# Triangular inverse in a two-block transformer kernel: row-by-row part on blocks of 8 instead of 16, and one more doubling level

## The chip, the cores and the metric

The kernel runs on one core of one Trainium2 chip. The metric is device time in microseconds of one execution. Before the change the three timed runs took 1562.48, 1565.49 and 1566.18 us; their median, 1565.49 us, is the time to compare with. One more execution was profiled; all rows below are from it.

## The reference, cut to what matters

The reference runs two layers of one model and one layer of another over 256 tokens of width 1024, in float32: feed-forward blocks, a gated delta rule mixer (8 heads), a sliding-window attention, and a last mixer that joins windowed attention with a linear recurrence in two directions (8 heads). The gated delta rule solves a unit lower triangular system in each chunk:

```
L = jnp.where(strict, jnp.einsum("bhnid,bhnjd->bhnij", kb, k) * decay, 0.0)
rhs = jnp.concatenate([v * beta[..., None], kb * jnp.exp(g)[..., None]], axis=-1)
sol = lax.linalg.triangular_solve(L, rhs, left_side=True, lower=True,
                                  transpose_a=False, conjugate_a=False, unit_diagonal=True)
```

and the recurrence of the last mixer is a scan over time steps:

```
sa = jnp.einsum('dbhij,dbhj->dbhi', state, a_t)
state = (state * w_t[..., None, :] + sa[..., :, None] * b_t[..., None, :]
         + v_t[..., :, None] * k_t[..., None, :])
y = jnp.einsum('dbhij,dbhj->dbhi', state, r_t)
```

The kernel does both in chunks, and in both it needs the inverse of a unit triangular matrix: 128x128 in the first mixer, 64x64 in the last.

## The kernel before, in words

Weights arrive as 512 KB blocks on one DMA queue (line 173). ScalarE rounds each block to a high part (line 177), VectorE forms the rest (line 178), and TensorE multiplies with both parts, three products for one (lines 181 to 184). These projections are nearly all of TensorE's work.

A mixer runs as a set of generators. `chain` (first mixer, one for each group of four heads) and `rw_chain` (last mixer, one for each pair of heads) hold the work in which each step waits for the one before; `stream` holds the projections. `weave` (lines 314 to 337) takes steps from both. A step yields two numbers: the TensorE time it takes, and the time until its result can be used. With these `weave` keeps a clock of its own and puts filler steps from the stream between a chain's step and its next one, until the clock has passed the second number times `slack`. In the last mixer TensorE's instructions keep exactly the order in which `weave` emits them (line 1510, slack 1.3, line 1511). In the first mixer (slack 1.1, line 792) a planner orders all engines by priority, and everywhere it orders VectorE and ScalarE. Each engine works its queue in order.

`tri_inverse` (lines 422 to 488) inverts eight triangular matrices at once, `nu = 8`, all four 32-row strips of the partitions side by side. It is called by `chain` twice in all and by `rw_chain` four times. Before the call ScalarE gathers the diagonal 32x32 blocks into `Lc` (lines 708 and 1196). Then:

- Lines 429 to 431: VectorE masks out the diagonal 16x16 blocks of `Lc` and adds the two halves, which gives `Ld`, 16 columns for each partition.
- Lines 433 to 440: the row-by-row part. For each row k a shuffle spreads row k of the block to its partitions (`irow`, line 438), a multiplication by the rows already found goes into `unit` (tile `iun`, line 439), and a reduction adds up (`iYc`, line 440). `unit` holds 1 + 2 + ... + 16 = 136 columns for each matrix; `inverse_scratch` fills it once for each mixer (line 419). All three operations grow with k.
- Lines 441 to 444: `iYc` is spread back into the diagonal blocks of `Y`, `Xt` is its transpose, and the step yields (0, 14.0).
- Lines 446 to 462: the doubling level from 16 to 32, on TensorE: 32 products `Lc`*`Y` into a bank, a masked copy `T` on VectorE (line 451), 64 products with `Xt` and `T`, and the two updates of `Y` and `Xt` on VectorE (lines 460 and 461).
- Lines 464 to 488: the level from 32 to 64, with ScalarE doing the copies.

A 32x32 float32 product shows in the profile as two matmul records and two weight loads. All matmuls of `mm` carry line 197 in the profile, whoever calls it.

The last mixer's head pairs overlap: the chain of pair t+1 prepares its operands (lines 1133 to 1139) while pair t inverts and scans.

Of the kernel before, what the change touches and what calls it, by code (L numbers as in the profile page):

```python
# [12 lines left out]
ALU = mybir.AluOpType  # L13
PSUM = bass.MemoryType.PSUM

P = 128
# [41 lines left out]
def _consts():  # L58
    i = np.arange(P)
    t, s = i[:, None], i[None, :]  # L60
    f = lambda m: m.astype(np.float32)


    half = np.concatenate([t // 16 % 2 == 0, t // 16 % 2 == 1], 1)
    unit = np.zeros((P, 136))
    for k in range(16):
        unit[:, k * (k + 1) // 2 + k] = i % 16 == k
    lev4 = (t % 32 < 16) & (np.arange(32)[None, :] >= 16)
    inv = [("half", f(half)), ("nhalf", -f(half)), ("lev4", f(lev4)), ("unit", unit)]
    groups = {  # L70
        "base": [("ident", f(t == s)), ("ones", np.ones((P, P), np.float32))],
        "delta": [("tri", f(t <= s)), ("maskA", np.where(s < t, NEG, 0.0)), ("maskL", np.where(s >= t, -NEG, 0.0))],
        "inv": inv,

        "swa": [("band", np.concatenate([np.where(s > t, 0.0, NEG), np.where(s <= t, 0.0, NEG)], 1))],

        "gqa": [(f"near{m}", np.where(np.abs(t + m * P - np.arange(256)[None, :]) <= P, 0.0, NEG)) for m in range(2)],
    }


    blk = t // 64 == s // 64
    groups["prep"] = [("triF", f(blk & (t <= s))), ("triB", f(blk & (t >= s))), ("sel", f(blk)[:, 0:65:64])]
    rw = []
    for d in range(2):
        m = np.zeros((P, 2, P), np.float32)
        for step in range(2):
            odd = step if d == 0 else 1 - step
            direct = np.arange(P) // 64 == odd
            at = np.where(direct | (d == 1), np.arange(P) % 64, 63 - np.arange(P) % 64)
            if d == 1:  # L90
                at = 63 - at
            m[:, step] = np.where(direct[None, :], at[:, None] <= at[None, :], at[:, None] < at[None, :])
        rw.append((f"m{d}", m.reshape(P, 2 * P)))
    groups["scan"] = rw
    half = 8
    inv = np.power(np.float32(500000.0), -np.arange(half, dtype=np.float32) * np.float32(2.0) / np.float32(16))
    ang = np.arange(256, dtype=np.float32)[:, None] * inv[None, :].astype(np.float32)
    cos, sin = np.cos(ang.astype(np.float32)), np.sin(ang.astype(np.float32))
    groups["gqa"] += [("cos", cos.reshape(2, P, half).transpose(1, 0, 2).reshape(P, 16)),
                      ("sin", sin.reshape(2, P, half).transpose(1, 0, 2).reshape(P, 16))]  # L100
    arrays, cols = {}, {}
    for g, parts in groups.items():
        at = 0
        for name, m in parts:
            cols[name] = (g, at, m.shape[1])
            at += m.shape[1]
        arrays["c_" + g] = np.ascontiguousarray(np.concatenate([m for _, m in parts], axis=1).astype(np.float32))
    return arrays, cols


CONSTS, CONST_COLS = _consts()


# [5 lines left out]
def _program(ctx, tc, a, out, stages):  # L119
    nc = tc.nc  # L120
# [10 lines left out]
    def bank(pool=None):  # L131
        pool = pool or psB
        return pool.tile([P, 512], F32, tag="A" if pool is psA else "B", name="bank")
# [17 lines left out]
    def C(name):  # L151
        g, o, n = CONST_COLS[name]
        return cst[g][:, o:o + n]
# [42 lines left out]
    def mm(o, lhsT, rhs, start=True, stop=True, **kw):  # L196
        nc.tensor.matmul(o, lhsT, rhs, start=start, stop=stop, **kw)  # L197
# [217 lines left out]
    q32 = [slice(32 * r, 32 * r + 32) for r in range(4)]  # L415

    def inverse_scratch(tl, nu):
        un = tl([nu, 136], "iun")
        nc.vector.tensor_copy(un, C("unit").unsqueeze(1).to_broadcast([P, nu, 136]))
        return un  # L420

    def tri_inverse(tl, Lc, off, nu, sign, unit, X, ydst=None):
        W = nu * 32
        uv = lambda y: y.rearrange("p (u s) -> p u s", u=nu)
        uf = lambda y: y.rearrange("p u s -> p (u s)")
        halves = lambda y: y.rearrange("p u (a s) -> p u a s", a=2)
        grid = lambda m: C(m).unsqueeze(1).unsqueeze(3).to_broadcast([P, nu, 2, 16])
        op = ALU.subtract if sign > 0 else ALU.add
        Lm, Ld = tl([nu, 32], "iLm"), tl([nu, 16], "iLd")
        nc.vector.tensor_tensor(halves(Lm), halves(Lc), grid("nhalf" if sign > 0 else "half"), ALU.mult)  # L430
        nc.vector.tensor_tensor(Ld, Lm[:, :, 0:16], Lm[:, :, 16:32], ALU.add)

        Yc = tl([nu, 16], "iYc")
        for k in range(16):
            o = k * (k + 1) // 2
            if k:
                row = tl([nu, 16], "irow", 2)[:, :, 0:k]
                nc.vector.stream_shuffle(row, Ld[:, :, 0:k], [i // 16 * 16 + k for i in range(32)])  # L438
                nc.vector.tensor_tensor(unit[:, :, o:o + k], row, Yc[:, :, 0:k], ALU.mult)
            nc.vector.tensor_reduce(Yc[:, :, k], unit[:, :, o:o + k + 1], mybir.AxisListType.X, ALU.add)  # L440
        Y, Xt = tl([nu, 32], "iY"), tl([nu, 32], "iX")
        nc.vector.tensor_tensor(halves(Y), Yc.unsqueeze(2).to_broadcast([P, nu, 2, 16]), grid("half"), ALU.mult)
        nc.vector.transpose(uf(Xt), uf(Y))
        yield 0, 14.0

        ps = bank()
        for u in range(nu):
            for r in q32:
                mm(ps[r, u * 32:u * 32 + 32], Lc[r, u], Y[r, u])
        T = tl([nu, 32], "iT")  # L450
        nc.vector.tensor_tensor(T, uv(ps[:, :W]), C("lev4").unsqueeze(1).to_broadcast([P, nu, 32]), ALU.mult)
        yield 0.15 * nu, 1.6
        ps = bank()
        for u in range(nu):
            for r in q32:
                mm(ps[r, u * 32:u * 32 + 32], Xt[r, u], T[r, u])
        for u in range(nu):
            for r in q32:
                mm(ps[r, W + u * 32:W + u * 32 + 32], T[r, u], Xt[r, u])
        nc.vector.tensor_tensor(Y, Y, uv(ps[:, :W]), op)  # L460
        nc.vector.tensor_tensor(Xt, Xt, uv(ps[:, W:2 * W]), op)
        yield 0.3 * nu, 1.6

        low, high = q32[0::2], q32[1::2]
        T = tl([nu, 32], "iT")
        ps = bank()
        for u in range(nu):
            for l, h in zip(low, high):
                mm(ps[l, u * 32:u * 32 + 32], off(u, h, l), Y[h, u])
        for l in low:  # L470
            nc.scalar.copy(T[l], uv(ps[l, :W]))
        for i, r in enumerate(q32):
            c = slice(i % 2 * 32, i % 2 * 32 + 32)
            nc.scalar.copy(X[r, :, c], Xt[r])
            if ydst:
                nc.scalar.copy(ydst(r)[:, :, c], Y[r])
        yield 0.08 * nu, 1.6
        ps = bank()
        for u in range(nu):
            for l, h in zip(low, high):  # L480
                mm(ps[h, u * 32:u * 32 + 32], T[l, u], Xt[l, u])
                if ydst:
                    mm(ps[l, u * 32:u * 32 + 32], Xt[l, u], T[l, u])
        for l, h in zip(low, high):
            nc.scalar.activation(X[h, :, 0:32], uv(ps[h, :W]), AF.Copy, scale=-float(sign))
            if ydst:
                nc.scalar.activation(ydst(l)[:, :, 32:64], uv(ps[l, :W]), AF.Copy, scale=-float(sign))
        yield 0.1 * nu, 1.6


    def deltanet():
# [4 lines left out]
        with tc.tile_pool(name="delta", bufs=1) as dp:  # L496
# [78 lines left out]

            conv = V("conv").rearrange("p (t j) -> p t j", j=4)
            unit = inverse_scratch(tl, 8)
            X64 = [tl([8, 64], f"X64{i}") for i in range(2)]
            Yf = [tl([8, P], f"Yf{i}") for i in range(2)]
# [123 lines left out]
            def chain(s):  # L703
# [3 lines left out]
                for r in q32:  # L707
                    nc.scalar.copy(Lc[r], L4[r, :, r])
                X, Y = X64[gr], Yf[gr]
                lo, hi = slice(0, 64), slice(64, P)  # L710
                yield from tri_inverse(tl, Lc, lambda u, h, l: L4[h, u, l], 8, 1, unit, X,
                                       lambda r: Y[r, :, (lo if r.start < 64 else hi)])
                ps = bank()
# [260 lines left out]
    def mixer2_body(tl, hT, rstd, sums, finish_norm):  # L974
# [71 lines left out]
        def rw_chain(t):  # L1046
# [146 lines left out]
            for r in q32:  # L1193
                for par in range(2):
                    Md = M[int(r.start // 64 == par)]
                    nc.scalar.copy(L4[r, :, par::2], Md[r, :, par::2, r])
            state["rw"][t] = 1
            yield from tri_inverse(tl, Lc, lambda u, h, l: M[int(h.start // 64 == u % 2)][h, u // 4, u % 4, l], 8, -1, unit,
                                   X64[t % 2])
            X = X64[t % 2]  # L1200
# [531 lines left out]
```

## Time and profile before

| what | before |
|---|---|
| median of 3 runs | 1565.49 us |
| the profiled execution's own time | 1568.78 us |
| its span (first to last instruction) | 1567.0 us |
| TensorE busy | 1510.5 us (96%) |
| VectorE busy | 1101.2 us (70%) |
| ScalarE busy | 918.8 us (59%) |
| mean granted TensorE clock | 0.984 |

A row of the timeline gives the start in us from the span's start, the time it took, engine, line, operation, what it writes and reads, shapes and the number of instructions merged; in brackets, for how long the engine had been idle before it and what ended that. PE is TensorE's matmul, PEld its weight load, DVE is VectorE, ACT is ScalarE, SPq the queue that issues the DMAs. Matmuls are pipelined, so a matmul's own time is longer than its distance to the next one; the distance is what it costs. "issue" stands for time in which an engine waited for nothing that the profile shows.

### The profile page before, as it was taken

What the parts mean: (1) busy time and instruction counts of PE and PEld (TensorE: products, weight loads), DVE (VectorE), ACT (ScalarE), POOL (GpSimd) and SP (SyncE); (2) the same over time, 40 slices, a digit from 0 to 9 for tenths busy, and PEclk for the clock granted to TensorE, in tenths of its full rate; (3) what the DMA queues carried; (4) which work ended last, traced back from release to release, by engine and by line L of the source; (5) the groups of instructions that cost most, each with busy time, mean ns of one, the idle gap of its engine ahead of it and who ended that gap; (6) DMA issues with size and microseconds to landing.
All of it is one profiled execution on the core that took longest, in us unless ns stands there. A gap on an engine that the chain in (4) does not pass through costs nothing.

```text
span 1567.0 us, 28074 instructions
## 1 busy us (share of the span) xinstructions
PE 1510.5 (96%) x10592; PEld 1298.8 (83%) x10592; DVE 1101.2 (70%) x2691; ACT 918.8 (59%) x2000; POOL 36.9 (2%) x51
## 2 busy tenths in 40 slices
PE   8999998999999999999999999999988988999998
PEld 6888887898888888888887888879977877778887
DVE  6766779686766667666666767667987865766665
ACT  6655576666655556555545655556767554655554
POOL 0000011011000000000100000000000000000000
PEclk9999998899999999999999999999999999999999
DMA  7766614243766647666432766646331222665551
GB/s 232 218 193 196 191 41 132 82 135 122 215 202 196 196 120 230 200 200 191 141 95 86 221 194 199 193 145 183 105 100 31 69 60 94 195 215 189 188 188 54
DMA packets 71192, 244.18 MB, mean 156 GB/s; under 512 B 8464, under 2 KB 12304, under 8 KB 71056
## 3 DMA queue, kind: packets, MB, share of 16 engines
q1 hardware_dynamic: 71056, 242.39, 51.0%
q8 instruction: 83, 1.36, 0.4%
q14 instruction: 53, 0.43, 0.1%
HBM read 241.31 MB, written 1.05 MB: 155 GB/s over the span
## 4 chain that ended last, share of the span: by engine, by line
PE 82%; DVE 9%; DMA 4%; ACT 3%; issue 1%; POOL 1%; SPq 0%; ACTq 0%; DVEq 0%; POOLq 0%
PE bank L189 22%; PE bank L197 12%; PE bank L182 12%; PE bank L184 12%; PE bank L183 11%; PE bank L190 11%; DVE wl L178 3%; DMA raw<-in_w_ff_dram 1%; ACT wh L177 1%; PE bank L248 1%; DMA raw<-in_ffn_w_dram 1%; DVE cacc L596 1%; DMA raw<-in_w_rwkv_dram 0%; DVE irow L438 0%; PE bank L851 0%
## 5 line engine op out<-in xcount | busy, mean ns | idle before, releaser
L178 DVE TENSOR_TENSOR wl<-raw,wh 128x512 fp32r<-128x512 f32 (+1 forms) x714 | 574.7, 828 | 219.2 <-ACT wh L177 213.3
L177 ACT CAST wh<-raw 128x512 fp32r<-128x512 f32 (+1 forms) x714 | 497.0, 731 | 286.5 <-DMA raw<-in_ffn_w_dram 173.6
L189 PE MATMUL bank<-hT,wh 128*128 128x512 f32 x1664 | 587.7, 396 | 3.7 <-DVE hT L255 3.2
L190 PE MATMUL bank<-hT,wl 128*128 128x256 f32 x1664 | 463.3, 279 | 0.1
L189 PEld LDWEIGHTS bank<-hT,wh 128*128 128x128 f32 x1664 | 312.8, 188 | 77.7 <-DVE hT L255 5.7
L190 PEld LDWEIGHTS bank<-hT,wl 128*128 128x128 f32 x1664 | 313.6, 188 | 4.9 <-DVE wl L178 0.6
L182 PE MATMUL bank<-wh,aT 128*128 128x512 f32 x584 | 233.4, 400 | 5.5 <-ACT aT L216 5.2
L184 PE MATMUL bank<-wh,aT 128*128 128x512 f32 x584 | 229.3, 396 | 1.2 <-DVE aT L217 1.1
L183 PE MATMUL bank<-wl,aT 128*128 128x512 f32 x584 | 229.1, 392 | 0.0
L182 PEld LDWEIGHTS bank<-wh,aT 128*128 128x128 f32 x584 | 110.1, 189 | 32.0 <-ACT aT L216 8.3
L184 PEld LDWEIGHTS bank<-wh,aT 128*128 128x128 f32 x584 | 109.8, 188 | 29.2 <-DVE aT L217 3.7
L183 PEld LDWEIGHTS bank<-wl,aT 128*128 128x128 f32 x584 | 110.3, 189 | 19.9
L182 PE MATMUL bank<-hT,wh 128*128 128x256 f32 x384 | 115.9, 302 | 0.0
L184 PE MATMUL bank<-hT,wl 128*128 128x256 f32 x384 | 111.0, 291 | 1.7 <-DVE wl L178 1.7
L183 PE MATMUL bank<-hT,wh 128*128 128x256 f32 x384 | 111.2, 290 | 0.0
L402 ACT ACTIVATE gs<-gs 128x256 f32<-128x256 f32 x88 | 36.7, 417 | 86.5 <-DVE gs L401 86.5
L194 DVE TENSOR_TENSOR av<-av,bank 128x256 f32<-128x256 f32 x120 | 50.0, 418 | 43.9 <-ACT av L193 43.2
L184 PEld LDWEIGHTS bank<-hT,wl 128*128 128x128 f32 x384 | 74.6, 195 | 3.8 <-DVE wl L178 2.4
L182 PEld LDWEIGHTS bank<-hT,wh 128*128 128x128 f32 x384 | 74.9, 195 | 2.8 <-issue 1.5
L183 PEld LDWEIGHTS bank<-hT,wh 128*128 128x128 f32 x384 | 75.0, 195 | 2.4 <-issue 2.0
L216 ACT CAST aT<-av 128x256 fp32r<-128x256 f32 x120 | 48.6, 406 | 20.8 <-DVE av L1555 12.0
L197 PE MATMUL bank<-wh,hT 128*128 128x256 f32 x256 | 57.6, 306 | 2.1 <-DVE hT L255 2.1
(415 smaller groups left out, 1940.0 us busy)
## 6 DMA issues: line engine op xcount, KB each, us to landing
raw<-in_ffn_w_dram SPq DMA_DIRECT2D x264, 512.0 KB, 4.2
raw<-in_w_ff_dram SPq DMA_DIRECT2D x64, 512.0 KB, 4.3
raw<-in_a_w_qkv_dram SPq DMA_DIRECT2D x24, 512.0 KB, 3.8
raw<-in_w_gate_dram SPq DMA_DIRECT2D x16, 512.0 KB, 3.5
raw<-in_w_rwkv_dram SPq DMA_DIRECT2D x14, 512.0 KB, 3.5
raw<-in_b_w_qk_dram SPq DMA_DIRECT2D x10, 512.0 KB, 4.2
raw<-in_a_w_z_dram SPq DMA_DIRECT2D x8, 512.0 KB, 3.6
raw<-in_a_w_out_dram SPq DMA_DIRECT2D x8, 512.0 KB, 3.5
```

Of the source, the lines that this page charges most:

```text
L177: nc.scalar.copy(hi[:, c], raw[:, c])
L178: nc.vector.tensor_tensor(lo[:, c], raw[:, c], hi.bitcast(F32)[:, c], ALU.subtract)
L182: nc.tensor.matmul(o, l[0], r[0], start=start, stop=False, **kw)
L183: nc.tensor.matmul(o, l[0], r[1], start=False, stop=False, **kw)
L184: nc.tensor.matmul(o, l[1], r[0], start=False, stop=stop, **kw)
L189: nc.tensor.matmul(o, l[0], both, start=start, stop=False, skip_group_check=True)
L190: nc.tensor.matmul(o[:, 0:256], l[1], both[:, 0:256], start=False, stop=stop, skip_group_check=True)
L194: nc.vector.tensor_tensor(t, t, o[:, 0:256], ALU.add)
L197: nc.tensor.matmul(o, lhsT, rhs, start=start, stop=stop, **kw)
L216: nc.scalar.copy(hi, src)
L248: nc.tensor.transpose(ps[:, q * 256 + h * P:q * 256 + (h + 1) * P], x[h][n][:, c * P:(c + 1) * P], ident)
L402: nc.scalar.activation(gs, gs, AF.Silu)
```

## The change: blocks of 8 row by row, and the doubling level run twice

The row-by-row part stops at row 7, with 36 columns of `unit` instead of 136. `Ld` is made by one reduction over four masked quarters instead of an addition of two halves. The doubling level on TensorE becomes a loop over two masks: `lev3` joins 8x8 blocks to 16x16, `lev4` joins 16x16 to 32x32 as before. Both use the same instructions. The first yield is (0, 7.5) instead of (0, 14.0). The constants have 108 columns instead of 172.

```
-        Lm, Ld = tl([nu, 32], "iLm"), tl([nu, 16], "iLd")
-        nc.vector.tensor_tensor(halves(Lm), halves(Lc), grid("nhalf" if sign > 0 else "half"), ALU.mult)
-        nc.vector.tensor_tensor(Ld, Lm[:, :, 0:16], Lm[:, :, 16:32], ALU.add)
-
-        Yc = tl([nu, 16], "iYc")
-        for k in range(16):
+        Lm, Ld = tl([nu, 32], "iLm"), tl([nu, 8], "iLd")
+        nc.vector.tensor_tensor(quarters(Lm), quarters(Lc), grid("nquart" if sign > 0 else "quart"), ALU.mult)
+        nc.vector.tensor_reduce(Ld, Lm.rearrange("p u (a s) -> p u s a", a=4), mybir.AxisListType.X, ALU.add)
+
+        Yc = tl([nu, 8], "iYc")
+        for k in range(8):
             o = k * (k + 1) // 2
             if k:
-                row = tl([nu, 16], "irow", 2)[:, :, 0:k]
-                nc.vector.stream_shuffle(row, Ld[:, :, 0:k], [i // 16 * 16 + k for i in range(32)])
+                row = tl([nu, 8], "irow", 2)[:, :, 0:k]
+                nc.vector.stream_shuffle(row, Ld[:, :, 0:k], [i // 8 * 8 + k for i in range(32)])
                 nc.vector.tensor_tensor(unit[:, :, o:o + k], row, Yc[:, :, 0:k], ALU.mult)
             nc.vector.tensor_reduce(Yc[:, :, k], unit[:, :, o:o + k + 1], mybir.AxisListType.X, ALU.add)
...
         nc.vector.transpose(uf(Xt), uf(Y))
-        yield 0, 14.0
-
-        ps = bank()
...
+        yield 0, 7.5
+
+        for lev in ("lev3", "lev4"):
+            ps = bank()
+            for u in range(nu):
+                for r in q32:
+                    mm(ps[r, u * 32:u * 32 + 32], Lc[r, u], Y[r, u])
+            T = tl([nu, 32], "iT")
+            nc.vector.tensor_tensor(T, uv(ps[:, :W]), C(lev).unsqueeze(1).to_broadcast([P, nu, 32]), ALU.mult)
+            yield 0.15 * nu, 1.6
+            ps = bank()
+            for u in range(nu):
+                for r in q32:
+                    mm(ps[r, u * 32:u * 32 + 32], Xt[r, u], T[r, u])
+            for u in range(nu):
+                for r in q32:
+                    mm(ps[r, W + u * 32:W + u * 32 + 32], T[r, u], Xt[r, u])
+            nc.vector.tensor_tensor(Y, Y, uv(ps[:, :W]), op)
+            nc.vector.tensor_tensor(Xt, Xt, uv(ps[:, W:2 * W]), op)
+            yield 0.3 * nu, 1.6
```

## Rows read from the trace of the kernel before

**Rows 1.** The page: busy time of each engine; shares of the chain of waits

```profile
PE 1510.5 (96%) x10592; PEld 1298.8 (83%) x10592; DVE 1101.2 (70%) x2691; ACT 918.8 (59%) x2000; POOL 36.9 (2%) x51
...
PE 82%; DVE 9%; DMA 4%; ACT 3%; issue 1%; POOL 1%; SPq 0%; ACTq 0%; DVEq 0%; POOLq 0%
```

**Rows 2.** Windows, first and last mixer: length, busy per engine, granted clock, DMA

```profile
196.00:330.00 134.00, 125.69 (x1406) 113.92 (x1406) 103.83 (x384) 89.19 (x175) 13.39 (x17) 0.92 0.31 94
...
1040.00:1330.00 290.00, 267.62 (x3173) 236.43 (x3174) 216.28 (x778) 175.72 (x433) 3.63 (x11) 0.95 0.30 92
```

**Rows 3.** Timeline of TensorE, the level of 16 in the first inverse

```profile
264.04 0.75 PE L197 MATMUL bank<-iY,Lc 32*32 32x32 f32 x64
...
264.72 0.38 PE L183 MATMUL bank<-hT,wh 128*128 128x256 f32 x1
...
265.86 0.72 PE L197 MATMUL bank<-iT,iX 32*32 32x32 f32 x62
...
267.08 0.38 PE L182 MATMUL bank<-hT,wh 128*128 128x256 f32 x1
```

**Rows 4.** Timeline of TensorE, the same level in the last mixer's third inverse

```profile
1229.35 0.74 PE L197 MATMUL bank<-iY,Lc 32*32 32x32 f32 x64 [0.51 <-DVE iY L442]
...
1234.70 1.08 PE L197 MATMUL bank<-iT,iX 32*32 32x32 f32 x64 [2.42 <-DVE nmean L1257]
...
1236.56 0.58 PE L197 MATMUL bank<-wh,sTh 128*128 128x256 f32 x1
```

**Rows 5.** Windows over the second set of products, columns as above

```profile
265.86:267.08 1.22, 1.22 (x130) 1.18 (x129) 1.22 (x3) 1.18 (x3) 0.00 (x0) 1.00 0.58 111
...
1234.70:1236.56 1.86, 1.86 (x128) 1.80 (x129) 1.86 (x5) 1.58 (x8) 0.00 (x0) 0.50 0.03 9
```

**Rows 6.** Timeline of TensorE, last mixer's first, second and fourth inverse

```profile
1141.41 0.39 PE L197 MATMUL bank<-wl,hT 128*128 128x256 f32 x1 [3.62 <-DVE wl L178]
...
1189.89 1.08 PE L197 MATMUL bank<-iT,iX 32*32 32x32 f32 x64 [1.54 <-DVE iT L451]
...
1273.52 0.74 PE L197 MATMUL bank<-iY,Lc 32*32 32x32 f32 x64 [2.54 <-DVE iY L442]
```

**Rows 7.** Timeline of TensorE, first mixer, stops named issue

```profile
270.38 0.37 PE L197 MATMUL bank<-iY,GL 32*32 32x32 f32 x10 [1.39 <-issue]
...
295.94 0.53 PE L197 MATMUL bank<-iX,iT 32*32 32x32 f32 x20 [0.96 <-issue]
```

**Rows 8.** The page, DMA queues: packets, MB, share of 16 engines

```profile
q8 instruction: 83, 1.36, 0.4%
```

**Rows 9.** Timeline of VectorE, rows 12 and 13 of an inverse

```profile
1127.80 0.29 DVE L438 STREAM_SHUFFLE irow<-iLd 128x104 f32<-128x104 f32 x1
1127.97 0.24 DVE L439 TENSOR_TENSOR iun<-irow,iYc 128x96 f32<-128x96 f32 x1
1128.14 0.16 DVE L210 TENSOR_TENSOR rsq<-rsq 128x10 f32<-128x10 f32 x1
...
1128.29 0.25 DVE L440 TENSOR_REDUCE iYc<-iun 128x8 f32<-128x104 f32 x1
```

**Rows 10.** Groups by line, VectorE, 1110 to 1285 us: busy, mean ns, idle before

```profile
L451 DVE TENSOR_TENSOR iT<-bank,c_inv 128x256 f32<-128x256 f32 x4 | 1.7, 413 | 0.5 <-PE bank L197 0.5
...
L1256 DVE TENSOR_REDUCE nmean<-bank 128x4 f32<-128x256 f32 x3 | 1.3, 419 | 2.1 <-PE bank L197 2.1
```

**Rows 11.** Timeline, start of the last mixer

```profile
1053.75 1.37 DVE L419 COPY iun<-c_inv 128x1088 f32<-128x1088 f32 x1
...
1056.16 0.50 PE L197 MATMUL bank<-wh,hT 128*128 128x256 f32 x2 [0.81 <-DVE hT L255]
```

**Rows 12.** Timeline of TensorE, first mixer, products of two sizes

```profile
288.42 0.33 PE L197 MATMUL bank<-T,X 64*64 64x64 f32 x2
...
288.67 0.24 PE L197 MATMUL bank<-iY,Lc 32*32 32x32 f32 x2
288.85 0.33 PE L197 MATMUL bank<-T,X 64*64 64x64 f32 x2
```

More of the change, by code (lines that the diff above doesn't have):

```diff
@@ L61, in _consts @@
     f = lambda m: m.astype(np.float32)
-    half = np.concatenate([t // 16 % 2 == 0, t // 16 % 2 == 1], 1)
-    unit = np.zeros((P, 136))
-    for k in range(16):
-        unit[:, k * (k + 1) // 2 + k] = i % 16 == k
-    lev4 = (t % 32 < 16) & (np.arange(32)[None, :] >= 16)
-    inv = [("half", f(half)), ("nhalf", -f(half)), ("lev4", f(lev4)), ("unit", unit)]
+    quart = np.concatenate([t // 8 % 4 == q for q in range(4)], 1)
+    unit = np.zeros((P, 36))
+    for k in range(8):
+        unit[:, k * (k + 1) // 2 + k] = i % 8 == k
+    c32 = np.arange(32)[None, :]
+    lev3 = (t % 16 < 8) & (c32 % 16 >= 8) & (t % 32 // 16 == c32 // 16)
+    lev4 = (t % 32 < 16) & (c32 >= 16)
+    inv = [("quart", f(quart)), ("nquart", -f(quart)), ("lev3", f(lev3)), ("lev4", f(lev4)), ("unit", unit)]
     groups = {
@@ L417, in inverse_scratch @@
     def inverse_scratch(tl, nu):
-        un = tl([nu, 136], "iun")
-        nc.vector.tensor_copy(un, C("unit").unsqueeze(1).to_broadcast([P, nu, 136]))
+        un = tl([nu, 36], "iun")
+        nc.vector.tensor_copy(un, C("unit").unsqueeze(1).to_broadcast([P, nu, 36]))
         return un
@@ L425, in tri_inverse @@
         uf = lambda y: y.rearrange("p u s -> p (u s)")
-        halves = lambda y: y.rearrange("p u (a s) -> p u a s", a=2)
-        grid = lambda m: C(m).unsqueeze(1).unsqueeze(3).to_broadcast([P, nu, 2, 16])
+        quarters = lambda y: y.rearrange("p u (a s) -> p u a s", a=4)
+        grid = lambda m: C(m).unsqueeze(1).unsqueeze(3).to_broadcast([P, nu, 4, 8])
         op = ALU.subtract if sign > 0 else ALU.add
-        Lm, Ld = tl([nu, 32], "iLm"), tl([nu, 16], "iLd")
-        nc.vector.tensor_tensor(halves(Lm), halves(Lc), grid("nhalf" if sign > 0 else "half"), ALU.mult)
-        nc.vector.tensor_tensor(Ld, Lm[:, :, 0:16], Lm[:, :, 16:32], ALU.add)
-        Yc = tl([nu, 16], "iYc")
-        for k in range(16):
+        Lm, Ld = tl([nu, 32], "iLm"), tl([nu, 8], "iLd")
+        nc.vector.tensor_tensor(quarters(Lm), quarters(Lc), grid("nquart" if sign > 0 else "quart"), ALU.mult)
+        nc.vector.tensor_reduce(Ld, Lm.rearrange("p u (a s) -> p u s a", a=4), mybir.AxisListType.X, ALU.add)
+        Yc = tl([nu, 8], "iYc")
+        for k in range(8):
             o = k * (k + 1) // 2
             if k:
-                row = tl([nu, 16], "irow", 2)[:, :, 0:k]
-                nc.vector.stream_shuffle(row, Ld[:, :, 0:k], [i // 16 * 16 + k for i in range(32)])
+                row = tl([nu, 8], "irow", 2)[:, :, 0:k]
+                nc.vector.stream_shuffle(row, Ld[:, :, 0:k], [i // 8 * 8 + k for i in range(32)])
                 nc.vector.tensor_tensor(unit[:, :, o:o + k], row, Yc[:, :, 0:k], ALU.mult)
@@ L441, in tri_inverse @@
         Y, Xt = tl([nu, 32], "iY"), tl([nu, 32], "iX")
-        nc.vector.tensor_tensor(halves(Y), Yc.unsqueeze(2).to_broadcast([P, nu, 2, 16]), grid("half"), ALU.mult)
+        nc.vector.tensor_tensor(quarters(Y), Yc.unsqueeze(2).to_broadcast([P, nu, 4, 8]), grid("quart"), ALU.mult)
         nc.vector.transpose(uf(Xt), uf(Y))
-        yield 0, 14.0
-        ps = bank()
[L447 to L462, printed above, removed]
+        yield 0, 7.5
[17 more added lines that the diff above has]
+            yield 0.3 * nu, 1.6
         low, high = q32[0::2], q32[1::2]
```

## The prediction

> **What bounds the kernel now.** I read the page's busy line first. TensorE is busy 1510.5 us of the 1567.0 us span, and 82% of the chain of waits that ended last is TensorE, 9% VectorE [rows 1]. So the kernel as a whole is bound by TensorE: work that is added there costs its full length unless TensorE would have stood still, and work that is taken from VectorE gains only what TensorE waits for it.
>
> Then the stretches. The triangular inverse runs six times: twice in the first mixer, four times in the last one. These two stages hold TensorE's idle time: 134.0 - 125.7 = 8.3 us in the first, 290.0 - 267.6 = 22.4 us in the second [rows 2]. Their mean granted clock is 0.92 and 0.95, so part of each runs at the lower of the two levels, 1.2 GHz: in the second stage 0.05 x 2 x 290 = 29 us, which costs 14.5 us. What the change can win lies in these 31 us of idle time and in that clock. What it costs is TensorE time.
>
> Then the timeline around single inverses. In the first one TensorE does not stand still at all: the products run between projections [rows 3]. In the last mixer each of the four inverses has a wait that ends on VectorE: 3.62 us in the first inverse (TensorE stood before a projection whose split weights were late, because VectorE had fallen behind), 1.54 us in the second, 0.51 and 2.42 us in the third, 2.54 us in the fourth [rows 4, 6]. That is 10.6 us.
>
> **The change part by part.**
>
> *TensorE, added.* The 16x16 doubling level is run a second time, for 8x8. A level is 32 products L*Y, then after VectorE 64 products X*T and T*X. Each product shows as two records. The first set of 64 records starts at 264.04 and the next matmul at 264.72: 0.68 us. The second set of 128 starts at 265.86 and the next matmul at 267.08: 1.22 us at full clock [rows 3, 5]. In the third inverse of the last mixer the second set took 1236.56 - 1234.70 = 1.86 us, at a granted clock of 0.50 [rows 4, 5]. So a level costs 1.90 to 2.54 us, and six cost 11.4 to 15.2 us. I take three of each: 13.3 us. None of it is hidden, as TensorE is the bound; where it falls into a wait, that is counted with the waits.
>
> *VectorE, removed.* Rows 8 to 15 of the row-by-row part go: 8 x 3 instructions in each inverse. In a busy stretch a shuffle starts 0.17 us before the next instruction, a multiply 0.17, a reduction 0.18 (the last from its own length of 0.25 less the overlap of the two others): some 0.5 us for a row near 12 [rows 9]. Widths grow evenly with the row, so I use that as the mean: 4.0 us less in an inverse.
>
> *VectorE, added.* Three 128x256 operations (T, Y, X) of 0.41 us each [rows 10], and the block sum Ld as a strided reduction instead of an addition. The nearest reduction of 256 elements took 0.42 us [rows 10]; the addition took part of that, so I put 0.1 to 0.4 more. With some overlap, 1.2 us. Net VectorE gives back 2.8 us per inverse, 17 us in all.
>
> *What that is worth.* Only the waits on VectorE shrink, each by no more than itself and by no more than 2.8: 2.8 + 1.54 + 2.8 + 2.54 = 9.7 us. Against it stands the planned distance: the generator now yields 7.5 instead of 14.0, which at a slack of 1.3 puts the first products 8.5 us earlier in TensorE's fixed order, so that less projection work lies in front of them; VectorE's queue still holds the next head pair's operations ahead of T. I take 8.0 of the 9.7; the low end is 3.
>
> *New waits.* The added level brings two more hand-overs to VectorE and back for each inverse. TensorE waits in order, so everything behind the waiting product waits too: projections, and the scan of the head pair before. With filler work between, such a hand-over cost nothing (264.72 to 265.86 is filled by projections [rows 3]); with VectorE behind it cost 1.54 to 2.42 us [rows 4, 6]. Six inverses at 0 to 2.4 us: 0 to 14. Since VectorE is less far behind I stay near the lower row: 2.0 us.
>
> *Issue.* In both inverses of the first mixer TensorE stopped in the middle of the small products with nothing that the profile shows as a cause, 1.39 and 0.96 us [rows 7]. The instruction queue brought 83 packets for 2 x 10592 records, 255 for a packet [rows 1, 8]; the change adds 6 x 384 = 2304, nine packets more. I take one more such stop, 1.2 us; the bounds are 0 and nine of 1.39, 12.5 us. The Trainium skill ("Runtime: NRT & Kernel Launch", section "Instruction fetch mechanics") holds that blocks of instructions are fetched ahead while the current one runs and that a crossing is mostly hidden. By that rule this term would be nothing and the sum 1.2 us lower; the two stops do not contradict it outright, as no row names the fetch as their cause.
>
> *The constants.* The copy that spreads the unit rows shrinks from 1088 to 288 elements per partition. In the last mixer it held VectorE for 1.37 us ahead of the normalised activations, for which TensorE then waited 0.81 us [rows 11]. At a quarter of the length that wait goes: 0.8 us. Copy and constants in the first mixer end before anything waits for them: nothing.
>
> *Clock.* Fewer long waits should mean less time at 1.2 GHz; more small products with hand-overs could mean more. Of the 14.5 us I give back 1.7, with the ends 6.8 less and 6.8 more.
>
> *Sum.* 13.3 + 2.0 + 1.2 - 8.0 - 0.8 - 1.7 = 6.0 us more. The profiled execution took 1568.8 us (span 1567.0 and 1.8 around it), 3.3 us above the median of the three runs, 1565.5. So 1574.8 on the profiled execution's scale, **1571.5 us** on the median's.
>
> **The rivals.**
>
> *Relief wins (faster).* VectorE is what holds the last mixer: all 9.7 us of waits go, the clock comes back with them (6.8), the copy's 0.8 too, the products run at full clock, and new hand-overs are covered: 11.4 - 9.7 - 0.8 - 6.8 = -5.9, 1559.6 us. For it: VectorE is busy 216.3 of 290.0 us there and each of the four inverses has its wait. Against it: 8.5 us less filler in front of the first products, and two more hand-overs. It decides from the point at which the waits and clock regained exceed 11.4 us.
>
> *A wash.* The products run at full clock, the hand-overs are covered, relief, copy and clock as in my sum: 11.4 - 8.0 - 0.8 - 1.7 = 0.9, 1566.4 us. For it: the first inverse shows a level that is wholly covered [rows 3].
>
> *New waits (much slower).* Each added level meets a wait like the second inverse's 1.54 us and runs at half clock, two more issue stops come, and half the relief is eaten: 15.2 + 9.2 + 2.4 - 4.9 - 0.8 = 21.1, 1586.6 us. For it: three of the last mixer's four inverses had a wait of 1.5 us or more at or near this very hand-over. Against it: VectorE has less to do.
>
> *Mixed sizes in the first mixer (slower).* There the planner orders TensorE, and it once wove 32x32 products with 64x64 ones of the other group: a pair of each took 288.85 - 288.42 = 0.43 us [rows 12], 16 records of the small kind alone would be 0.17. Eight such pairs cost up to 3.2 us over the plain order. With one more level in both groups, two more such stretches: 6.0 + 6.4 = 12.4, 1577.9 us. The Trainium skill ("TensorEngine Tiling (Array Packing)", "Tiling Modes") says that a change of tiling mode drains TensorE; the 0.43 us agrees with that.
>
> **How the numbers follow.** Forecast 0.30, relief 0.24, a wash 0.28, new waits 0.13, mixed sizes 0.05. What a measurement of this kernel can tell from no change is about 0.3%, 4.7 us: 1560.8 to 1570.2. So faster 0.24, same 0.28, slower 0.48. The range reaches to 1554 (relief with the low end of the unknown costs) and to 1586 (most of the new waits); the forecast's own is 1570 to 1577.
>
> **What would show it.** Right: TensorE's records rise by 1152; VectorE's busy time falls by some 17 to 30 us; the two stages of [rows 2] have more TensorE busy time by 11 to 15 us; the waits on VectorE before the first products and T are under 1.5 us each; the copy of unit rows is under 0.5 us. Wrong: TensorE's idle time in the last mixer falls by more than 12 us (relief), or the second hand-over shows waits over 1.5 us in most inverses (new waits), or the clock of that stage moves by more than 0.03.

## The result: 22 to 25 us slower

| | before | after |
|---|---|---|
| median of the runs | 1565.6 us | 1590.3 us (1587.2 to 1591.5) |
| ratio, with its 95% interval | | 1.0143 [1.0121, 1.0166] |
| span of the profiled execution | 1567.0 us | 1588.6 us |
| TensorE / VectorE busy | 1510.5 / 1101.2 us | 1528.2 / 1086.6 us |
| mean granted TensorE clock | 0.984 | 0.981 |

The forecast was 1571.5 us, its range ended at 1586. The two medians lie 24.7 us apart; the recorded ratio, 1.0143, gives a little less. From here on a kernel's distance from the one before is (ratio - 1) x 1565.5, in the experiments with the ratio taken against runs of the kernel before on the same chip: the changed kernel stands at +22.4 us [18.9, 26.0].

The page after, answering [rows 1, 8]: busy time of the engines, instruction queue (packets, MB, share), chain of waits.

```profile
PE 1528.2 (96%) x11744; PEld 1313.4 (83%) x11744; DVE 1086.6 (68%) x2517; ACT 918.8 (58%) x2000; POOL 37.9 (2%) x51
...
q8 instruction: 92, 1.51, 0.4%
...
PE 79%; DVE 10%; DMA 5%; ACT 4%; issue 2%; POOL 1%; SPq 0%; ACTq 0%; DVEq 0%; POOLq 0%
```

TensorE has the 1152 records that were forecast and 17.7 us more busy time; the queue brought the nine packets more. VectorE's busy time fell by 14.6 us. Yet VectorE's share of the chain rose from 9 to 10%, and "issue" from 1 to 2%.

Where the time went: I take ScalarE's first square of x as the start of the last mixer and the first transpose of gt as its end. Windows over that stretch, and over most of the first mixer (columns as in [rows 2]); the kernel before first.

```profile
196.00:430.00 234.00, 223.35 (x1973) 198.05 (x1973) 177.26 (x548) 153.65 (x330) 21.60 (x26) 0.96 0.40 120
1042.80:1319.20 276.40, 254.09 (x3109) 225.33 (x3107) 206.08 (x763) 171.55 (x427) 3.63 (x11) 0.96 0.29 89
```

The same windows of the changed kernel:

```profile
196.00:430.00 234.00, 221.33 (x2292) 195.35 (x2292) 166.36 (x474) 147.97 (x317) 21.44 (x26) 0.93 0.35 109
1052.70:1341.20 288.50, 262.71 (x3875) 233.22 (x3874) 194.04 (x647) 170.82 (x427) 3.82 (x11) 0.95 0.28 85
```

The last mixer starts 9.9 us later, so that much was lost before it, in the first mixer. It takes 288.5 instead of 276.4 us: 8.6 us more TensorE busy time and 3.5 us more idle time, although VectorE does 12 us less. In the first mixer's window the granted clock is 0.93 where it was 0.96. Each such figure is one execution's: run 1 below has the changed kernel's first mixer unchanged, and its profile shows 0.95 there.

The first inverse, TensorE's timeline after (answers [rows 3, 7]; the bracket is the idle time before and its releaser):

```profile
257.67 0.75 PE L199 MATMUL bank<-iY,Lc 32*32 32x32 f32 x64
...
260.09 0.72 PE L199 MATMUL bank<-iT,iX 32*32 32x32 f32 x62
...
262.02 0.69 PE L199 MATMUL bank<-iX,iT 32*32 32x32 f32 x57 [1.14 <-issue]
...
265.62 0.60 PE L199 MATMUL bank<-k 128*128 128x128 f32 x4 [1.31 <-issue]
...
267.18 0.96 PE L199 MATMUL bank<-iT,iX 32*32 32x32 f32 x64
...
270.26 0.43 PE L199 MATMUL bank<-iX,iT 32*32 32x32 f32 x13 [1.42 <-issue]
```

And windows of the changed kernel around it:

```profile
260.00:265.00 5.00, 3.08 (x198) 2.87 (x199) 4.09 (x12) 2.12 (x3) 0.69 (x1) 1.00 0.71 206
265.00:270.00 5.00, 3.23 (x128) 2.96 (x127) 1.43 (x7) 1.15 (x3) 0.69 (x1) 0.74 0.45 151
270.00:275.00 5.00, 4.74 (x61) 4.10 (x62) 4.05 (x27) 3.88 (x11) 0.00 (x0) 0.50 0.02 7
275.00:280.00 5.00, 5.00 (x78) 4.71 (x79) 1.33 (x8) 3.65 (x8) 0.00 (x0) 0.50 0.01 3
```

The first set of the added level takes 0.68 us, as one did before. The second is cut by a stop of 1.14 us in which the profile shows nothing that is waited for; two more stops follow within 8.3 us. TensorE is busy 6.3 of 10 us, and then runs at the lower of its two levels, 1.2 GHz, for the next 10 us, projections included (one of 128x256 every 0.21 us instead of 0.12).

TensorE's long waits in the last mixer after (answers [rows 4, 6]; first inverse, second, third, then three rows of the fourth):

```profile
1145.82 1.08 PE L199 MATMUL bank<-iY,Lc 32*32 32x32 f32 x64 [3.74 <-DVE iY L463]
...
1203.62 1.07 PE L199 MATMUL bank<-iT,iX 32*32 32x32 f32 x64 [2.46 <-ACT sTh L1381]
...
1236.84 1.08 PE L199 MATMUL bank<-iY,Lc 32*32 32x32 f32 x64 [2.52 <-DVE iY L444]
...
1287.28 0.74 PE L199 MATMUL bank<-iY,Lc 32*32 32x32 f32 x64 [1.00 <-DVE iY L444]
1291.45 0.50 PE L199 MATMUL bank<-iX,iT 32*32 32x32 f32 x35 [1.41 <-issue]
1299.38 0.48 PE L199 MATMUL bank<-UV,M 128*64 128x64 f32 x3 [2.46 <-issue]
```

VectorE just ahead of the first of these waits:

```profile
1144.68 0.42 DVE L1141 TENSOR_TENSOR AR<-kn,cen 128x256 f32<-128x256 f32 x1
1145.02 0.42 DVE L1142 TENSOR_TENSOR kd<-kd,p_r 128x256 f32<-128x256 f32 x1
1145.35 0.41 DVE L463 TENSOR_TENSOR iY<-iY,bank 128x256 f32<-128x256 f32 x1
```

The long waits are about as many as before, in other places. The 3.74 us stand at the new hand-over between the two levels: the products for Y ended at 1139.0, but its update starts at 1145.35, as it stands on VectorE behind a dozen operations of the next head pair. The wait in front of the first products, which VectorE's relief was to shorten, is there in the third and fourth inverse all the same.

### The profile page after: what moved, and what is told of

It reads as the page before. It is cut to its first block, busy times and chain, and to the rows that moved or that the text cites. A ratio compares the mean times of both kernels' runs of the same rounds, so it can differ in the third digit from the quotient of the medians.

```text
span 1588.6 us, 30234 instructions
## 1 busy us (share of the span) xinstructions
PE 1528.2 (96%) x11744; PEld 1313.4 (83%) x11744; DVE 1086.6 (68%) x2517; ACT 918.8 (58%) x2000; POOL 37.9 (2%) x51
## 4 chain that ended last, share of the span: by engine, by line
PE 79%; DVE 10%; DMA 5%; ACT 4%; issue 2%; POOL 1%; SPq 0%; ACTq 0%; DVEq 0%; POOLq 0%
PE bank L191 21%; PE bank L199 12%; PE bank L184 11%; PE bank L186 11%; PE bank L185 11%; PE bank L192 10%; DVE wl L180 3%; DMA raw<-in_ffn_w_dram 2%; ACT wh L179 1%; DMA raw<-in_w_ff_dram 1%; PE bank L250 1%; DVE cacc L599 1%; DMA raw<-in_w_rwkv_dram 0%; PE bank L854 0%; DVE hT L257 0%
```

## The experiments

My first theory was that the cost is TensorE's: the small products with their stops and the half clock behind them. The rivals: the smaller planned distance, and the hand-overs to VectorE. The first four runs split the change into its three parts.

**1. The distance, in the last mixer only.**

```diff
-        yield 0, 7.5
+        yield 0, 7.5 if sign > 0 else 14.0
```

> The changed kernel with the planned distance in front of the first products put back to 14.0 in the last mixer alone. Theory 'small products' (the cost is TensorE's own: six levels of 192 small products, the stops in which the profile shows nothing that is waited for, and the half clock behind them, wherever they stand): 1586 to 1594 us, about the 1590 of the changed kernel; the waits for iY and iT in the last mixer may fall by 2 to 4 us, no more. Rival 'distance' (the smaller distance puts the products too early, so that TensorE meets VectorE's results late): the last mixer gets back most of the 14 us that it lost, 1577 to 1581 us.

Measured: 1578.0 us, +11.4 [6.9, 16.1]; 11 us of the loss are gone, as the rival "distance" had it. TensorE's waits for the inverse's VectorE operations that are left in the last mixer (us in total, times, longest), and the window of the last mixer:

```profile
PE bank L199 <- DVE iT L454: 3.0, 2, 1.5
...
PE bank L199 <- DVE iY L444: 0.2, 1, 0.2
```

```profile
1051.60:1328.70 277.10, 257.78 (x3875) 229.83 (x3873) 193.31 (x647) 170.77 (x427) 3.79 (x11) 0.97 0.30 89
```

The last mixer takes 277.1 us, 0.7 more than before the change and 11.4 less than in the changed kernel, with all its added products.

**2. VectorE's relief alone, near distance.**

```diff
-        for lev in ("lev3", "lev4"):
+        for lev in ("lev4",):
```

> The changed kernel with its added level left out (the 8x8 blocks are not joined to 16x16, so that the inverse is not the reference's): VectorE's relief and the distance 7.5 remain, TensorE has the work of before. Theory 'small products': relief is worth little, as the waits that go come back elsewhere: 1560 to 1567 us. Rival 'relief is worth its 8 us, and the added level costs 33': 1555 to 1559 us. Rival 'distance': 1574 us or more.

Measured: 1565.4 us, -0.9 [-4.1, 2.3]. By itself this reads as "relief is worth little", which my theory said. The next run shows that it is the sum of two large terms.

**3. The distance alone.**

```diff
-        yield 0, 14.0
+        yield 0, 7.5
```

> The kernel before with the planned distance 7.5 in place of 14.0, nothing else. Theory 'small products': 1562 to 1570 us, the same or some 3 us more from the waits in front of the first products. Rival 'distance': 1575 us or more.

Measured: 1578.3 us, +10.6 [7.4, 13.9], with not one product or VectorE operation changed. The profiled execution, 1582.4 us, was the slowest of the ten, so its rows show the mechanism rather than the mean price. Its last mixer starts at 1041.8, 1.0 us earlier than before, and takes 290.6 us instead of 276.4: the cost lies in the last mixer. TensorE's two longest waits there (second: third inverse):

```profile
1130.46 1.08 PE L197 MATMUL bank<-iY,Lc 32*32 32x32 f32 x64 [7.04 <-DVE rsq L210]
...
1233.61 1.08 PE L197 MATMUL bank<-iY,Lc 32*32 32x32 f32 x64 [8.78 <-DVE iY L442]
```

VectorE meanwhile: start of the row-by-row part, row 8, the last row, and Y:

```profile
1222.05 0.28 DVE L431 TENSOR_TENSOR iLd<-iLm 128x128 f32<-128x128 f32 x1
...
1227.53 0.22 DVE L438 STREAM_SHUFFLE irow<-iLd 128x64 f32<-128x64 f32 x1
...
1232.80 0.29 DVE L440 TENSOR_REDUCE iYc<-iun 128x8 f32<-128x128 f32 x1
1233.13 0.42 DVE L442 TENSOR_TENSOR iY<-iYc,c_inv 128x256 f32<-128x256 f32 x1
```

TensorE came to the first products at 1233.61 - 8.78 = 1224.83, when the row-by-row part was 2.8 us old, and had to stand there, since its order is fixed. In the first mixer the near distance brings a wait of 3.8 us for wl, which the changed kernel and those of runs 1, 2, 4, 6, 7 and 9, all with 7.5 there, show too; the start of the last mixer, 1.0 us earlier, shows no loss from it here. Against this kernel, run 2 is 11.5 us faster: that is the relief at this distance.

**4. The level alone, near distance.** The level of 16 twice in the kernel before, with 7.5:

```diff
-        yield 0, 14.0
...
+        yield 0, 7.5
+
+        for _ in range(2):
...
```

> The kernel before with its one doubling level run twice (the second pass adds the same corner once more, so that the inverse is not the reference's) and the distance 7.5: the added level without VectorE's relief. Theory 'small products': 1588 to 1598 us, so that this kernel less the one before at the same distance is 23 to 29 us. Rival 'relief is worth its 8 us': 1597 to 1605 us. Should the level alone cost only its 13 us of TensorE time and the rest come from the distance or from VectorE's new order, 1576 to 1582 us.

Measured: 1604.6 us, +37.4 [30.8, 44.0]. The time is that of "relief is worth its 8 us"; the difference from run 3, 27 us, lies in the 23 to 29 of my theory. Step by step, +10.6 (distance) - 11.5 (relief) is run 2, and the level on top, +23.3, is the changed kernel. These are differences of successive runs, so that they must add up; in another order the terms differ (the level costs 27 without the relief, the relief is worth 15 with the level).

Its first mixer speaks against a fixed price of small products. It has as many of them as the changed kernel, and 92 packets too:

```profile
196.00:430.00 234.00, 221.34 (x2316) 195.43 (x2316) 175.87 (x545) 149.47 (x323) 22.08 (x26) 0.96 0.37 114
```

The clock is 0.96, as before the change, the stops named issue add up to 6.0 us in the whole kernel, and the last mixer starts 6.7 us later than in run 3.

**5. Relief at the far distance.** Run 2 with 14.0 in both mixers.

> The changed kernel with the added level left out (8x8 blocks not joined to 16x16, so that the inverse is not the reference's) and the distance put back to 14.0 in both mixers: VectorE's relief alone, at the distance of before. If relief is worth what it was at the near distance (12 to 13 us between the two kernels without and with it at 7.5): 1552 to 1556 us. If the distance had already bought most of it: the 8 us or less of the forecast, 1557 to 1563 us. If relief is worth nothing once the distance is right: 1564 to 1567 us.

Measured: 1548.9 us, -19.1 [-23.3, -14.7], more than any of the three cases. Its windows:

```profile
196.00:430.00 234.00, 226.15 (x2011) 199.80 (x2010) 177.85 (x496) 158.72 (x341) 22.34 (x26) 0.98 0.43 127
1035.20:1297.00 261.80, 246.64 (x3107) 219.43 (x3106) 189.41 (x635) 170.95 (x427) 3.63 (x11) 0.99 0.31 94
```

The last mixer is 14.6 us shorter than before: 7.2 of idle time and 7.4 of busy time with the same products, since the clock rises from 0.96 to 0.99. So the distance costs 18 us once the relief is there (run 2 less this one), and the relief is worth 19.1 us where TensorE doesn't come too early, against 11.5 where it does.

**6. The level's products with no hand-over.** Nothing reads what the added level computes; its second and third set take Y in place of T.

```diff
-            nc.vector.tensor_tensor(T, uv(ps[:, :W]), C(lev)...
+            if lev == "lev4":
+                nc.vector.tensor_tensor(T, uv(ps[:, :W]), C(lev)...
...
-            nc.vector.tensor_tensor(Y, Y, uv(ps[:, :W]), op)
+            if lev == "lev4":
+                nc.vector.tensor_tensor(Y, Y, uv(ps[:, :W]), op)
...
```

> The changed kernel, distance 7.5, in which the added level still issues its three sets of 32 products but nothing reads them (VectorE's T, Y and X of that level are left out, so that 8x8 blocks are not joined): the products with no hand-over. Beside it stand 1565.4 us without the level and 1590.3 us with all of it. Theory 'small products' (the level costs through TensorE: its records, stops and half clock): 1583 to 1592 us. Rival 'hand-overs' (only the products' own 11 to 15 us without the hand-overs, the rest is waits on VectorE): 1575 to 1581 us.

Measured: 1585.4 us, +15.5 [12.1, 18.9]: 16.4 over run 2, and 7 us under the changed kernel. Products cost 16; hand-overs, with VectorE's three operations for each inverse, 7. The last mixer of run 2, then of this run:

```profile
1038.30:1316.70 278.40, 258.16 (x3108) 228.65 (x3107) 190.79 (x635) 170.62 (x427) 3.64 (x11) 0.93 0.29 88
1056.80:1335.20 278.40, 256.18 (x3874) 227.68 (x3872) 190.23 (x635) 170.54 (x427) 3.64 (x11) 0.98 0.29 88
```

In these two executions it is equally long: the products of four of the six levels lengthened nothing there, and all that they cost stands ahead of it: the last mixer starts at 1056.8 instead of 1038.3, 18.5 us later. The changed kernel, with the hand-overs, reaches its last mixer 4.1 us sooner than this one and needs 10.1 us more for it.

**7. The same TensorE time in large products.**

```diff
+            if lev == "lev3":
+                for j in range(2):
+                    mm(ps[:, 0:256], uf(Lc)[:, 0:128], uf(Y))
+            else:
...
+                for j in range(3):
+                    mm(ps[:, 0:256], uf(Xt)[:, 0:128], uf(Y))
```

> As the kernel with the added level's products alone (1585.4 us; nothing reads them, blocks of 8 are not joined), but in place of the level's 96 small products stand five products of 128x128 by 128x256 that nothing reads, two where L*Y was and three where X*T and T*X were: some 2 us of TensorE time for each inverse as before, in a tenth of the instructions. Theory 'the smallness' (stops between small products and the half clock behind them are what makes the level dearer than its length): the clock and the idle time of the kernel with the level left out, 1565.4 + 11 to 14 = 1576 to 1580 us. Rival 'TensorE's time is time' (the extra 20 us come from where the work stands, whatever its size): 1583 to 1588 us.

Measured: 1570.6 us, +5.3 [2.2, 8.3], even less than "the smallness" said. The replaced level in its first inverse, and what follows:

```profile
258.59 1.10 PE L199 MATMUL bank<-iY,Lc 128*128 128x256 f32 x4
259.75 1.46 PE L199 MATMUL bank<-iY,iX 128*128 128x256 f32 x6
261.14 0.75 PE L199 MATMUL bank<-iY,Lc 32*32 32x32 f32 x64
```

Its starts take 2.55 us, of which 0.22 belong to two other products between them (left out here): 2.3 us, more than the 1.9 us of the small products. Its first mixer in windows, whole and around the inverses:

```profile
196.00:430.00 234.00, 223.23 (x1994) 196.68 (x1993) 173.37 (x485) 155.28 (x333) 21.45 (x26) 0.97 0.40 121
255.00:305.00 50.00, 47.60 (x866) 41.88 (x865) 32.27 (x97) 32.76 (x70) 1.39 (x2) 0.93 0.38 119
```

The same of run 6, with small products:

```profile
196.00:430.00 234.00, 220.72 (x2283) 196.23 (x2282) 162.78 (x465) 146.61 (x315) 21.44 (x26) 0.91 0.35 106
255.00:305.00 50.00, 45.04 (x1064) 39.99 (x1062) 25.56 (x89) 22.85 (x46) 1.39 (x2) 0.70 0.33 105
```

The granted clock is 0.93 against 0.70 in these 50 us (0.73 in the changed kernel and 0.83 in run 1, whose first mixers are the same program, so that such a figure differs by 0.1 from one execution to the next). The last mixer starts at 1044.9 here and at 1056.8 in run 6: the whole difference of 10 us lies ahead of it. The stops named issue add up to 9.8 us in run 6, 1.6 us here, 2.8 us in run 2, with no added level at all.

**8. Fewer small products in the kernel before.** Xt is the transpose of Y, so VectorE can make it from Y in place of T*X and a subtraction.

```diff
-        for u in range(nu):
-            for r in q32:
-                mm(ps[r, W + u * 32:W + u * 32 + 32], T[r, u], Xt[r, u])
...
-        nc.vector.tensor_tensor(Xt, Xt, uv(ps[:, W:2 * W]), op)
+        nc.vector.transpose(uf(Xt), uf(Y))
```

> The kernel before with the products T*X of its doubling level replaced by a transpose of the updated Y on VectorE (the same Xt, one VectorE operation for another): 6 x 32 products fewer on TensorE. Theory 'small products' (what small products cost is their own time and the stops in the middle of long runs of them): 6 x 0.6 = 3.7 us and up to two of the stops of 1.0 to 1.4 us go, 1558 to 1563 us. Rival 'VectorE leads' (the hand-overs set the time, so that what TensorE saves becomes a wait): 1564 to 1568 us.

Measured: 1568.5 us, +0.6 [-2.2, 3.4]. "VectorE leads" was right here: TensorE is busy 1503.3 us, 7.2 less, and not faster. With its one level per inverse the kernel before doesn't pay for these products.

**9. The same edit in both levels of run 1.**

> The changed kernel with distance 14.0 in the last mixer (1578.0 us as run above), and in both levels the products T*X replaced by a transpose of Y on VectorE: 12 x 32 products fewer than there. Theory 'small products': 12 x 0.6 = 7.3 us of TensorE go, and in the first mixer one or two of the three stops with the half clock behind them, 2 to 7 us: 1564 to 1570 us. Rival 'VectorE leads': 1575 to 1580 us.

Measured: 1567.1 us, -1.7 [-4.1, 0.6]: 13 us less than run 1, more than the 7.3 us of products that the edit takes out by the reckoning in the expectation. Its last mixer is 8.8 us shorter than that of before and starts 4.2 us later, so that the first mixer still loses. That pointed to the next run.

**10. The old inverse in the first mixer, the new one with far distance and transposes in the last** (both sets of constants and both functions in one kernel; in the last mixer, the function of run 9).

> The first mixer with the inverse of before (blocks of 16), the last mixer with blocks of 8, distance 14.0, and transposes in place of T*X in both of its levels. If the two mixers add up as their stages did in the runs above (first mixer 0, last mixer -8.8 us): 1556 to 1561 us, faster than both kernels. If what the last mixer gained there hung on the first mixer's state (weights that wait in their buffers, the clock): 1563 to 1568 us.

Measured: 1556.6 us, -10.2 [-14.1, -6.3]: faster than both kernels. Two rows of TensorE's waits in its last mixer, at the inverse:

```profile
PE bank L206 <- DVE iT L535: 3.0, 2, 1.5
...
PE bank L206 <- issue: 1.5, 1, 1.5
```

Of the waits in front of the first products and between the levels none over 0.3 us is left.

**11. Run 9 with distance 10.0 in the first mixer.**

> The kernel with transposes and distance 14.0 in the last mixer (1567.1 us as run above), with distance 10.0 in place of 7.5 in the first mixer too. Theory 'distance counts in both mixers': the wait of 3.8 us before the first inverse's products goes, 1562 to 1565 us. Rival 'in the first mixer the distance is free': 1566 to 1568 us.

Measured: 1562.6 us, -4.7 [-8.1, -1.3]. The wait of 3.8 us for wl is gone (0.8 is left), as expected, but the interval overlaps with that of run 9: a gain of some 3 us is likely, not shown. The added level with 14.0 in the first mixer wasn't tried.

**12. Run 10 with distance 18.0 in the last mixer.**

> The kernel with the old inverse in the first mixer and the new one in the last, distance 18.0 in place of 14.0 in the last mixer. If the last mixer's VectorE waits (3 us before T) still shrink with distance: 2 to 3 us less than its twin with 14.0. If 14.0 already covers the row-by-row part: within 1.5 us of its twin, or more, as the chains end later.

Measured: 1563.4 us, -3.6 [-7.7, 0.3]; 7 us more than its twin with 14.0, on the same chip; its fastest of ten executions, 1559.6 us, is slower than the slowest of the twin's five, 1558.1. Too far costs as well; the profiled execution (span 1570.8 us) lies well above the median, so I don't read a cause from it.

## Why the prediction was wrong

**The planned distance: the step that failed.** The prediction saw that the first products move 8.5 us forward in TensorE's order, and priced that at the 1.7 us between "9.7" and "8.0". It costs 10.6 us by itself (run 3), 18 us once the relief is there (run 5 against 2), and in the changed kernel 11.0 us from the last mixer alone (run 1), of the 16.4 us by which the forecast of 6.0 was short. What the runs showed in place of a small loss: TensorE comes to the first products before Y is there, stands for up to 8.8 us since its order is fixed, and the last mixer's clock falls too (0.96 to 0.92 in run 3). My own numbers spoke against that price: a relief of "2.8 us per inverse" can't make up for 8.5 us of lost lead. Every wait from which I subtracted was read from a trace in which that lead was there.

**Relief: mis-sized the other way.** 8.0 + 0.8 + 1.7 = 10.5 us for relief, copy and clock; measured 11.5 us at the near distance, 19.1 at the far one. For the waits alone 8.0 was near, 7.2 us of idle time in the last mixer; what was mis-sized is the clock that comes back with them, 7.4 us there against the 1.7 reckoned, and the first mixer, for which I had put nothing: in run 5 the last mixer starts 7.6 us earlier than before. Its length was low as well: rows 8 to 15 took 1227.53 to 1233.09, 5.6 us in which VectorE did nothing else (run 3), against the 4.0 reckoned. Busy time fell by 14.6 us, under the 17 to 30 that I had named, in small part since the block sum is dearer: 614 ns for a reduction whose price I took from one of 419.

```profile
L454 DVE TENSOR_TENSOR iT<-bank,c_inv 128x256 f32<-128x256 f32 x8 | 3.4, 421 | 3.0 <-PE bank L199 3.0
...
L433 DVE TENSOR_REDUCE iLd<-iLm 128x64 f32<-128x256 f32 x4 | 2.5, 614 | 0.1
```

(The changed kernel's VectorE groups in the last mixer: busy, mean ns, idle before. The T, at 421 ns, was priced rightly.)

**The level's products: 13.3 + 1.2 us, measured 16.4 (run 6).** The sum is nearly right, for a wrong reason. "None of it is hidden, as TensorE is the bound" failed: the last mixer holds four of the six levels and is no longer with them than without (run 6 against 2), and 14 us of TensorE time in large products, six times 2.3, cost 6 (run 7). What is paid for stands in the first mixer: stops (in the whole kernel 3.2 us before, 8.7 us after, within "0 and 12.5") and the half clock behind them. My clock term was for the last mixer, where the clock went from 0.96 to 0.95; the first mixer's, for which I had none, went from 0.96 to 0.93 of 234 us, an estimated 7 us (2 us by run 1's 0.95). That stops and half clock came with the small products in these places is shown by runs 6 and 7. Which of the two brings the other is not, and run 4, whose first mixer has as many of these products and stands at 0.96 as before, shows that the price hangs on where they stand. Nor did TensorE "not stand still at all" in the first inverse, as the prediction has it: that holds for the rows in [rows 3], but the stop of 1.39 us in [rows 7] stands in the same inverse.

**New waits: 2.0 us, measured 7 (run 6 against the changed kernel, VectorE's added operations included),** inside 0 to 14. The longest wait at a new hand-over is the one of 3.74 us; most inverses show none over 1.5 us there, which was my mark for the rival.

**Copy: right.** It took 0.31 us instead of 1.37, and the waits for hT in the last mixer fell from 2.1 to 0.9 us, 1.2 where 0.8 was reckoned.

**The rivals.** "New waits", 1586.6 us, came nearest in time, with a chance of 0.13. Its half clock and its two more stops are there; its hand-overs are the smaller part, and the relief was eaten by the distance, not by them. "Relief wins" was near with relief and clock, 17.3 us against 19.1 in run 5, but lacked the distance and had the level at 11.4 us instead of 23.3.

"Mixed sizes" [rows 12] came half true: where the kernel before has one stretch of pairs, the changed kernel has two, the second at half clock. The second pair of the first stretch starts at 281.89 and that of the second at 288.00, 0.43 and 0.64 us after the first:

```profile
281.46 0.33 PE L199 MATMUL bank<-Yf,GL 64*64 64x64 f32 x2
281.72 0.24 PE L199 MATMUL bank<-iY,Lc 32*32 32x32 f32 x2
...
287.36 0.47 PE L199 MATMUL bank<-T,X 64*64 64x64 f32 x2
287.76 0.31 PE L199 MATMUL bank<-iT,iX 32*32 32x32 f32 x2
```

One more stretch is 3.2 us by the prediction's own price, which is too high, since it left out the larger products' own time (16 records of them alone took 1.04 us before the change, from 304.49 to 305.53). It isn't what makes the first mixer dear: run 6, whose last mixer starts latest, has one stretch as before.

None of the three signs that were to show the prediction wrong came: the last mixer's idle time rose by 3.5 us, its clock moved by 0.01, and most hand-overs were short. The distance had no sign of its own. How near the sum would have come without it is open, as the added level with 14.0 in both mixers wasn't run: run 1, with 14.0 in the last mixer, stands at +11.4 us against my +6.0. That it is no further off is luck: the relief was worth 8.6 us more than reckoned and the level cost 6.8 us more, two errors that offset each other in the sum.

**The stops.** Stops stand mostly in the runs of small records, and grow from 3.2 to 8.7 us with packets of the instruction queue from 83 to 92 (10.3 us in run 1 and 6.0 in run 4, at 92 as well); with the level in 60 records they are 1.6 us at 83 packets. The Trainium skill ("Runtime: NRT & Kernel Launch", section "Instruction fetch mechanics") holds that the crossing of a block of instructions is mostly hidden; by that rule stops of this length would not come from crossings. No row names the fetch as their cause, so the rule is not refuted, but it is no ground for a price of nothing.

## What to carry to other kernels

Where an engine's order is fixed by planned distances, a changed distance is an edit of its own: price it first, by asking at what time the engine will now come to the wait and when the other one will be done. A term near zero in an experiment (run 2) may be two of 11 us; vary one part at a time before calling it nothing. Read the price of added work stage by stage: the same products cost nothing in the last mixer and more than their length in the first. And a run of hundreds of small products can be dearer than its length: count the stops in it and the clock behind it, and look for the product that a transpose can replace.

## What the runs showed of the hardware

- Five products of 128x128 by 128x256 in f32 took 2.3 us by their starts at full clock (run 7); the 96 products of 32x32 that they replaced took 1.9 us, and the kernel with them took 10 us more (run 6).
- In the changed kernel's first inverse the granted clock fell to 0.50 behind 10 us of small products and stops in which TensorE was busy for 6.3 us, and was 0.50 for the next 10 us although TensorE was busy 4.7 and 5.0 us of the two stretches of 5 us. Run 4, with as many small products placed otherwise, stood at 0.96 over the window of its first mixer (the changed kernel: 0.93).
- Transposing Xt out of Y on VectorE took 7.2 us of TensorE time from the kernel before and nothing from its time (run 8), but, done in both levels, 13 us from the kernel of run 1 (run 9 against it): what such an edit is worth hangs on what its stage waits for.
